# Mixer A's values in plain float32, in pairs of 64-column products, two bursts a unit

## The chip, the cores and the metric

The kernel runs on one core of a Trainium2 chip. The metric is the device time of one execution in microseconds. The engines are TensorE (PE in the profile, with its weight loads as PEld), VectorE (DVE), ScalarE (ACT), GpSimd (POOL) and SyncE (SP, which issues most of the DMAs).

## What is computed

One layer of a hybrid attention model: a normalized and modulated input, one input projection, two attention mixers with eight query heads each (two key/value heads, so a group of four query heads shares one), gates, one output projection and a residual. 1024 latent tokens attend in blocks of 128 queries; 128 context tokens attend to themselves. Cut to the two mixers for latent tokens:

```python
def global_attn_latent(q, k_lat, v_lat, k_ctx, v_ctx):            # mixer A
    k_all = jnp.concatenate([k_ctx, k_lat], axis=1)               # 128 + 1024 keys
    v_all = jnp.concatenate([v_ctx, v_lat], axis=1)
    def one_block(qblk):                                          # 128 queries
        s = jnp.einsum('bqkgd,bskd->bkgqs', qblk, k_all).astype(jnp.float32) * (d ** -0.5)
        p = jax.nn.softmax(s, axis=-1).astype(v_all.dtype)
        return jnp.einsum('bkgqs,bskd->bqkgd', p, v_all)
...
# mixer B: the same over a window of 128 to each side and the context keys, with a sink logit a head
...
def merge_out(o_a, g_a, o_b, g_b, w_out):
    return jnp.concatenate([o_a * jax.nn.silu(g_a), o_b * jax.nn.silu(g_b)], axis=-1) @ w_out
```

Everything is float32.

## The kernel before

Most matmuls here are in float32r, the type of reduced precision. To keep the result near float32, an operand is kept in two float32r parts, a high one (the rounded value) and a low one (what the rounding left); a product then takes three matmuls (high x high, high x low, low x high).

The first 310 us make the modulation (float32 matmuls in 32-column tiles, line 375), the projections, the rotated and normalized queries (stored in DRAM) and the keys and values, which stay in SBUF. `v_hi[:, m]` holds the high parts of mixer m's values, 64 columns a key block and head group; beside them stand 64 columns of ones for mixer A and the low parts for mixer B. `v_lo` holds mixer A's low parts (`put_values`, `split_values`).

Then comes attention, in 36 units `(t, m, g)`: query tile t, mixer m, head group g, in the order A, B, A, B of each tile; units 32 to 35 are the context ("prompt") tile, last of all. A latent unit of mixer A has nine key blocks, one of the prompt has one; a unit of mixer B has three or four. One block is one slot of a list, written out by hand; the main loop takes a slot an iteration and emits, in this order: what was put off to it (`later(n, f)` puts f n iterations on; `tick` runs it), the scores of the slot, row-maximum matmuls (`pmx`, line 941) or mixer B's score matmuls (`sn`) of a coming unit, some output-projection matmuls (`po`, line 1313, 2.5 a slot from the queue `outq`), and the value products of the slot three back (`LAG`). Each engine runs its instructions in the order of emission.

For a mixer A block, `scores` makes `st` (128 keys x 4 heads x 128 queries) in PSUM with two matmuls, its exponentials `pe` on ScalarE, their high part `ph` on ScalarE (line 1221) and the low part `pl` on GpSimd (line 1225; block 4 on VectorE, line 1223). `values` then adds to the unit's PSUM tile `pv` three matmuls of 512 columns (lines 1235, 1237, 1238): values beside ones x `ph`, low values x `ph` into the upper 64 partitions only, values beside ones x `pl`. So partitions 0 to 63 of `pv` have the weighted values, partitions 64 to 127 the softmax sum. After a unit's last block, iterations later by `END_AT`: `inverse` (ScalarE: log and exponential, which gives 1 over the sum), `gated` (VectorE multiplies by it in two 64-partition halves, GpSimd by the gate tile `sgl`), `parts` (the two float32r parts of the result for the output projection). Mixer B's weights are transposed on TensorE (line 1212), and its value products are two matmuls a block.

Of the kernel before, what the change touches and what calls it, by code (L numbers as in the profile page):

```python
# [18 lines left out]
P = 128  # L19
D = 1024  # L20
KT = D // P
HD = 64
# [11 lines left out]
PROMPT_AT = 32  # L34
KS = (0, 1, 4, 5, 2, 3, 6, 7)
PL_DVE = (4,)
# [48 lines left out]
PROMPT_PV = "CCAC"  # L85
PROMPT_PL = ()
LOW_DVE = (-2, -1)
# [11 lines left out]
VC_AT = 4  # L99
# [31 lines left out]
def hybrid_step(ctx, tc, x_prompt, x_sample, cache_k_a, cache_v_a, cache_k_b, cache_v_b,  # L131
# [18 lines left out]
    def later(n, f):  # L150

        agenda.setdefault(now[0] + n, []).append(f)
# [13 lines left out]
    def bank(tag, name):  # L166
        return ps.tile([P, 512], F32, tag=tag, name=name, bufs=BANKS[tag])
# [604 lines left out]
    def split_values(src, j):  # L772

        nc.vector.tensor_tensor(v_lo[:, j : j + 2, :], src[:, 0], v_hi[:, 0, j : j + 2, 0, :], op=ALU.subtract)
        nc.vector.tensor_tensor(v_hi[:, 1, j : j + 2, 1, :], src[:, 1], v_hi[:, 1, j : j + 2, 0, :], op=ALU.subtract)

    with tc.tile_pool(name="kt", bufs=2) as kt:
        W_GB.pools[WRAW : WRAW + 2] = [(kt, 2)] * 2
        sg_tile.append(lambda n: kt.tile([P, 512], F32, tag="kh", name=n))
        for b in range(0, 20, 4):  # L780
            later(4 + b // 2, lambda b=b: nc.gpsimd.tensor_scalar(
                v_hi[:, 0, b : b + 4, 1, :], gain4, 0.0, 1.0, op0=ALU.mult, op1=ALU.add))
        ones = ident_r.bitcast(F32)[64:68].unsqueeze(1)
        for out, n in ((kla[64:68].rearrange("p g b n -> p (g b) n"), 18), (klp[64:68, 0:2], 2)):
            later(ONES_AT, lambda out=out, n=n: nc.vector.tensor_scalar(
                out, ones.to_broadcast([4, n, P]), 0.0, 1.0, op0=ALU.mult, op1=ALU.add))
# [39 lines left out]

        def put_values(src, t):
            j = 2 * t if t else 18
            nc.scalar.copy(v_hi[:, :, j : j + 2, 0, :], src)
            later(1, lambda: split_values(src, j))  # L830

        def key(pk, t, idx):
# [45 lines left out]
                f()  # L878

        put_keys(kc, 0, 0, "c", CACHE_AT)  # L880
        later(VC_AT, lambda: nc.scalar.copy(v_hi[:, :, 0:2, 0, :], vc))
# [296 lines left out]
    def blocks(t, m, g):  # L1178

        if t == 0:  # L1180
            k = (khp[:, g, :], klp[0:68, g, :]) if m == 0 else 0
            return [(k, v_hi[:, m, 18 + g], v_lo[:, 18 + g, :])]
        if m == 0:
            return [((kha[:, g, b, :], kla[:, g, b, :]), v_hi[:, 0, 2 * b + g], v_lo[:, 2 * b + g, :]) for b in range(9)]
        p0, p1_ = window(t)
        at = {p: b + 1 for b, p in enumerate(POS)}
        return [(p - p0, v_hi[:, 1, 2 * at.get(p, 0) + g], None) for p in range(p0, p1_)]

    pvb, og = {}, {}
    nsl = [0]  # L1190
# [2 lines left out]
    def load_gate(i):  # L1193
        if i < NU:
            t, m, g = units[i]
            sgl[i] = w2.tile([P, 2, P], F32, tag="sgl", name=f"sgl{i}")
            h0 = HD * (8 * m + 4 * g)
            nc.sync.dma_start(
                sgl[i], g_dram[h0 : h0 + 4 * HD, P * place(t) : P * place(t) + P].rearrange("(c p) n -> p c n", p=P))

    def parts_tiles(i, b):
        return [w3.tile([P, 512], F32R, tag=n, name=f"{n}{i}_{b}") for n in ("ph", "pl")]

    def scores(i, b, blk):

        t, m, g = units[i]
        s = bank("B", f"st{i}_{b}")
        ph, pl = parts_tiles(i, b)
        if m == 1:
            o = P * blk[0]  # L1210
# [6 lines left out]
        nc.tensor.matmul(s, kh, qtile[i], start=True, stop=False)  # L1217
# [3 lines left out]
        nc.scalar.copy(ph, pe)  # L1221
        if (i - PROMPT_AT in PROMPT_PL) if t == 0 else b in PL_DVE:
            later(1, lambda: nc.vector.tensor_tensor(pl, pe, ph, op=ALU.subtract))
        else:
            nc.gpsimd.tensor_tensor(pl, pe, ph, op=ALU.subtract)  # L1225
        return ph, pl

    def values(i, b, last, blk, ph, pl):
        t, m, g = units[i]
        _, vh, vl = blk  # L1230
        if b == 0:
            pvb[i] = bank(PROMPT_PV[i - PROMPT_AT] if t == 0 else "C", f"pv{i}")
        pv = pvb[i]
        two = vh.rearrange("p s d -> p (s d)")
        nc.tensor.matmul(pv, two, ph, start=(b == 0), stop=False)  # L1235
        if m == 0:
            nc.tensor.matmul(pv[0:64, :], vl, ph, start=False, stop=False)  # L1237
        nc.tensor.matmul(pv, two, pl, start=False, stop=last)  # L1238
        if not last:
            return  # L1240

        v = {}

        def inverse():
            v["rs"] = w2.tile([64, 512], F32, tag="rs", name=f"rs{i}", bufs=1)
            if m == 1:
                nc.scalar.copy(v["rs"], pv[64:128, :])
                return
            nc.scalar.activation(v["rs"], pv[64:128, :], AF.Ln)
            nc.scalar.activation(v["rs"], v["rs"], AF.Exp, scale=-1.0)  # L1250

        def gated():
            rs = v["rs"]
            o = 768 + 256 * (i % 3)
            of = spare[0][:, o : o + 256].rearrange("p (c n) -> p c n", c=2)
            pvv = pv[0:64, :].rearrange("p (c s n) -> p c s n", s=2, n=P)
            srv = rs.rearrange("p (c s n) -> p c s n", s=2, n=P)
            for s in range(2):
                nc.vector.tensor_tensor(of[64 * s : 64 * s + 64], pvv[:, :, s, :], srv[:, :, s, :],
                                        op=ALU.add if m else ALU.mult)  # L1260
            nc.gpsimd.tensor_tensor(of, of, sgl.pop(i), op=ALU.mult)
            later(GATE_LATE, lambda: load_gate(i + 2))
            v["of"] = of

        def parts():
            while held[0] == NOG:
                outq.pop(0)()
            held[0] += 1
            oh = ogp.tile([P, 2, P], F32R, tag="ogh", name=f"ogh{i}")
            ol = ogp.tile([P, 2, P], F32R, tag="ogl", name=f"ogl{i}")  # L1270
            nc.scalar.copy(oh, v["of"])  # L1271
            og[t, 2 * m + g] = oh, ol
            eng = nc.vector if i - PROMPT_AT in LOW_DVE else nc.gpsimd
            later(1, lambda: eng.tensor_tensor(ol, v["of"], oh, op=ALU.subtract))

        ends = PROMPT_END if t == 0 else END_AT if i < PROMPT_AT - 2 else LAST_END
        for n, f in zip(ends, (inverse, gated, parts)):
            later(n, f)
        if m == 1:
            later(ends[3], lambda: outq.extend(out_items(t, g)))  # L1280

    po, yt, gt = {}, {}, {}

# [78 lines left out]
    credit, live = 0.0, []  # L1362
    load_gate(0)
    load_gate(1)
    for s in range(len(slots) + LAG + PROMPT_END[3]):
        tick()
        if s < len(slots):
            live.append((slots[s], slots[s] and scores(slots[s][0], slots[s][1], slots[s][3])))
        for n, at in WO_LATE.items():
            if s == at:  # L1370
                load_wo(n, w2)
                later(3, lambda n=n: split_wo(n))
        for f in due.get(s, ()):
            f()
        for _ in range(LATE[s] if s < len(LATE) else 0):
            late_product(late.pop(0))
        rate = OUTRATE if s < start[PROMPT_AT - HELD] else END_RATE if s < start[PROMPT_AT] else PROMPT_RATE
        credit = min(credit + rate, 6.0) if outq else 0.0
        while outq and credit >= 1.0:
            outq.pop(0)()  # L1380
            credit -= 1.0
        if s >= LAG and live:
            slot, parts = live.pop(0)
            if slot:
                values(*slot, *parts)
    for f in outq:
        f()
    in_order(tc)
# [62 lines left out]
```

## Time and profile before

| | |
|---|---|
| median of three runs | 704.2 us (704.17, 704.20, 704.34) |
| span of the profiled execution | 704.1 us; its own time isn't given apart from the three |
| TensorE busy | 691.6 us, 98% |
| VectorE, ScalarE, GpSimd busy | 443.3, 420.0, 342.3 us |
| attention, 310 to 680 us | TensorE busy 369.2 of 370 us |
| mean granted TensorE clock | 0.997 |

A matmul's time in the profile includes its way through the array, in which the next one already runs: a 512-column float32r matmul has 0.39 us, but the next starts 0.23 us after it. A float32 matmul leaves two records. Lines are those of the kernel before.

### The profile page before, as it was taken

What the parts mean: (1) busy time and instruction counts of PE and PEld (TensorE: products, weight loads), DVE (VectorE), ACT (ScalarE), POOL (GpSimd) and SP (SyncE); (2) the same over time, 40 slices, a digit from 0 to 9 for tenths busy, and PEclk for the clock granted to TensorE, in tenths of its full rate; (3) what the DMA queues carried; (4) which work ended last, traced back from release to release, by engine and by line L of the source; (5) the groups of instructions that cost most, each with busy time, mean ns of one, the idle gap of its engine ahead of it and who ended that gap; (6) DMA issues with size and microseconds to landing.
All of it is one profiled execution on the core that took longest, in us unless ns stands there. A gap on an engine that the chain in (4) does not pass through costs nothing.

```text
span 704.1 us, 10711 instructions
## 1 busy us (share of the span) xinstructions
PE 691.6 (98%) x3554; PEld 561.4 (80%) x3554; DVE 443.3 (63%) x991; ACT 420.0 (60%) x856; POOL 342.3 (49%) x364
## 2 busy tenths in 40 slices
PE   6999999999999999999999999999999999999997
PEld 2788988878788789986788888878888888887876
DVE  3555247875676873537677577667666775775564
ACT  4455411412233553389877877787788778877870
POOL 3457023332323241657857655755574557456742
PEclk9999999999999999999999999999999999999999
DMA  8960283348435015423222122121211231212324
GB/s 330 415 245 16 109 305 76 72 93 295 131 89 175 1 61 187 157 64 102 90 69 83 34 82 73 46 82 58 86 61 52 69 90 46 83 52 90 91 60 144
DMA packets 53447, 78.64 MB, mean 112 GB/s; under 512 B 6848, under 2 KB 25728, under 8 KB 52368
## 3 DMA queue, kind: packets, MB, share of 16 engines
q1 hardware_dynamic: 45360, 66.28, 27.8%
q10 hardware_dynamic: 8032, 11.68, 6.2%
q8 instruction: 28, 0.46, 0.3%
q14 instruction: 27, 0.22, 0.1%
HBM read 58.72 MB, written 19.21 MB: 111 GB/s over the span
## 4 chain that ended last, share of the span: by engine, by line
PE 88%; ACT 4%; DMA 2%; DVE 2%; issue 2%; ACTq 1%; SPq 0%; POOL 0%; DVEq 0%; POOLq 0%
PE po L1313 14%; PE pv L1238 6%; PE pv L1235 6%; PE pmx L941 5%; PE st L1217 4%; PE pv L1237 4%; PE st L1218 4%; PE pq L279 4%; PE pq L280 4%; PE pq L278 4%; PE st L1212 4%; PE pg L292 3%; PE pg L293 3%; PE pg L288 3%; PE pk L279 2%; PE pk L280 2%
## 5 line engine op out<-in xcount | busy, mean ns | idle before, releaser
L1225 POOL TENSOR_TENSOR pl<-pe,ph 128x512 fp32r<-128x512 f32 x130 | 167.9, 1294 | 141.9 <-DVE nm L1002 67.5
L942 DVE TENSOR_REDUCE mx<-pmx 128x1 f32<-128x384 f32 x192 | 101.4, 553 | 57.3 <-PE pmx L941 56.2
L1220 ACT ACTIVATE pe<-st 128x512 f32<-128x512 f32 x146 | 86.7, 594 | 27.1 <-PE st L1218 26.4
L1221 ACT CAST ph<-pe 128x512 fp32r<-128x512 f32 x146 | 90.6, 621 | 4.8
L1238 PE MATMUL pv<-pl,v_hi 128*128 128x512 f32 x208 | 82.5, 397 | 0.3 <-POOL pl L1225 0.3
L1235 PE MATMUL pv<-ph,v_hi 128*128 128x512 f32 x208 | 82.6, 397 | 0.0
L197 POOL TENSOR_TENSOR rs_q<-ms_q,mhalf 128x8 f32<-128x8 f32 x18 | 34.8, 1931 | 80.7 <-DVE ms_q L195 80.7
L1313 PE MATMUL po<-wo,ogh 128*128 128x512 f32 (+1 forms) x224 | 73.1, 387 | 0.0
L1002 DVE CUSTOM_DVE_ANT_0 sn<-sn,mask,nsink 128x512 f32<-128x512 f32 (+1 forms) x64 | 46.4, 724 | 41.0 <-PE sn L999 38.6
L941 PE MATMUL pmx<-kha,qt 128*128 128x384 f32 x192 | 61.0, 363 | 0.5 <-ACT pen L988 0.3
L1217 PE MATMUL st<-qt,kha 128*128 128x512 f32 x144 | 57.9, 402 | 0.1
L1237 PE MATMUL pv<-ph,v_lo 128*64 128x512 f32 x146 | 57.6, 395 | 0.0
L1218 PE MATMUL st<-qb,kla 68*128 68x512 f32 x144 | 57.1, 397 | 0.0
L1238 PEld LDWEIGHTS pv<-pl,v_hi 128*128 128x128 f32 x208 | 39.2, 188 | 17.3 <-POOL pl L1225 0.7
L988 ACT ACTIVATE pen<-sn,nm 128x512 f32<-128x512 f32 (+2 forms) x72 | 44.9, 625 | 5.8 <-DVE nm L1015 2.7
L1213 ACT CAST ph<-st 128x512 fp32r<-128x512 f32 x62 | 36.4, 587 | 19.7 <-PE st L1212 19.4
L1313 PEld LDWEIGHTS po<-wo,ogh 128*128 128x128 f32 x224 | 41.0, 188 | 6.2 <-ACT ogh L1271 0.3
L1235 PEld LDWEIGHTS pv<-ph,v_hi 128*128 128x128 f32 x208 | 39.3, 189 | 7.0 <-issue 0.3
L1313 PE MATMUL po<-wo,ogl 128*128 128x512 f32 (+1 forms) x112 | 43.2, 386 | 0.0
L1214 DVE TENSOR_TENSOR pl<-st,ph 128x512 fp32r<-128x512 f32 x62 | 42.4, 685 | 1.2 <-ACT ph L1213 0.7
L675 ACT ACTIVATE sqq<-pq 128x512 f32<-128x512 f32 x18 | 10.8, 598 | 53.3 <-PE pq L280 13.8
L941 PEld LDWEIGHTS pmx<-kha,qt 128*128 128x128 f32 x192 | 35.5, 190 | 6.4 <-DVE mx L942 1.2
(238 smaller groups left out, 1701.3 us busy)
## 6 DMA issues: line engine op xcount, KB each, us to landing
qt<-qd SPq DMA_DIRECT2D x36, 256.0 KB
wm<-in_w_mod_ss_dram SPq DMA_DIRECT2D x8, 1024.0 KB
qd<-qo0q ACTq DMA_DIRECT2D x36, 128.0 KB
qd<-qo1q ACTq DMA_DIRECT2D x36, 128.0 KB
sgl<-gd SPq DMA_DIRECT2D x36, 128.0 KB
out_dram<-yt SPq DMA_DIRECT2D x17, 256.0 KB
xn<-in_x_sample_dram SPq DMA_DIRECT2D x8, 512.0 KB
wg<-in_w_mod_g_dram SPq DMA_DIRECT2D x4, 1024.0 KB
```

The source lines that it names most:

```text
L941: nc.tensor.matmul(pm[:, 0:384], lhs, kha[:, g, 3 * b : 3 * b + 3, :], start=True, stop=True)
L942: nc.vector.tensor_reduce(mx[:, h, b : b + 1], pm[:, 0:384], axis=AX.X, op=ALU.max)
L1002: nc.vector.tensor_tensor_reduce(s, s, mask[:, m0 : m0 + n], -1.0, nsink[:, 4 * g + h : 4 * g + h + 1], op0=ALU.add, op1=ALU.min, accum_ou ...
L1217: nc.tensor.matmul(s, kh, qtile[i], start=True, stop=False)
L1218: nc.tensor.matmul(s, kl, qbtile[i], start=False, stop=True)
L1220: nc.scalar.activation(pe, s, AF.Exp)
L1221: nc.scalar.copy(ph, pe)
L1225: nc.gpsimd.tensor_tensor(pl, pe, ph, op=ALU.subtract)
L1235: nc.tensor.matmul(pv, two, ph, start=(b == 0), stop=False)
L1237: nc.tensor.matmul(pv[0:64, :], vl, ph, start=False, stop=False)
L1238: nc.tensor.matmul(pv, two, pl, start=False, stop=last)
L1313: nc.tensor.matmul(po[c], x, wo_parts[KT * n + k][lo][:, q], start=(k == KS[0] and p == 0), stop=(k == KS[-1] and p == 2))
```

## The change

Mixer A's values are kept as plain float32 (`v_all`), and a tile of ones beside them; mixer B's parts stay as they were. A mixer A block no longer splits its exponentials: `pe` (seven buffers instead of three) is the moving operand itself. Its value product is a pair of float32 matmuls with the same 64-column weights, one for heads 0 and 2 into partitions 0 to 63 and one for heads 1 and 3 into partitions 64 to 127 of `pv`, 256 columns each. The products of blocks 0 to 4 are emitted together two iterations after block 4's scores (`LAGA`), those of blocks 5 to 8 two after block 8's. The softmax sum is made apart: the blocks' exponentials are added up in a tile `acc` (GpSimd, the last add on VectorE), and one pair with ones as weights, at the end of the second burst, sums that over the keys into the other half of `pv`. So the sums stand on the same partitions as the values; `inverse` works on 128 x 256, GpSimd multiplies the gate by it, and one VectorE multiply of 128 x 256 makes the gated result. A prompt unit of mixer A has one burst of two pairs.

```diff
-PES = 3
+PES = 7
+SPLIT = 5
+LAGA = 2
+ENDA = (1, 3, 5)
+ACC_DVE = (8,)
...
-    v_hi = kv.tile([P, 2, 20, 2, HD], F32R, name="v_hi")
-    v_lo = kv.tile([P, 20, HD], F32R, name="v_lo")
+    v_all = kv.tile([P, 20, HD], F32, name="v_all")
+    v_hi = kv.tile([P, 20, 2, HD], F32R, name="v_hi")
+    ones = kv.tile([P, HD], F32, name="ones")
+    nc.gpsimd.memset(ones, 1.0)
...
+    def keep_values(src, j):
+
+        nc.scalar.copy(v_all[:, j : j + 2, :], src[:, 0])
+        nc.scalar.copy(v_hi[:, j : j + 2, 0, :], src[:, 1])
...
         nc.scalar.activation(pe, s, AF.Exp)
-        nc.scalar.copy(ph, pe)
-        if (i - PROMPT_AT in PROMPT_PL) if t == 0 else b in PL_DVE:
-            later(1, lambda: nc.vector.tensor_tensor(pl, pe, ph, op=ALU.subtract))
+        if b == 0:
+            acc[i] = pe
         else:
-            nc.gpsimd.tensor_tensor(pl, pe, ph, op=ALU.subtract)
-        return ph, pl
+            first = acc[i]
+            if b == 1:
+                acc[i] = w3.tile([P, 512], F32, tag="acc", name=f"acc{i}", bufs=1)
+            add = lambda: (nc.vector if b in ACC_DVE else nc.gpsimd).tensor_tensor(acc[i], first, pe, op=ALU.add)
+            if b in ACC_DVE:
+                later(1, add)
+            else:
+                add()
+        return pe
...
+    def burst(i, made, first, last):
+
+        if first:
+            pvb[i] = pv_bank(i)
+        pv = pvb[i]
+
+        def product(o, lhs, rhs, start, stop):
+            r = rhs.rearrange("p (c s n) -> p c s n", s=2, n=P)
+            for s in range(2):
+                nc.tensor.matmul(pv[HD * s : HD * s + HD, o : o + 256].rearrange("p (c n) -> p c n", c=2), lhs,
+                                 r[:, :, s, :], start=start, stop=stop)
+
+        for n, (blk, pe) in enumerate(made):
+            product(0, blk[1], pe, first and n == 0, False)
+        if not last:
+            return
+        product(256, ones, acc.pop(i), False, True)
+        v = {}
+
+        def inverse():
+            v["rs"] = w2.tile([P, 256], F32, tag="rsa", name=f"rs{i}", bufs=1)
+            nc.scalar.activation(v["rs"], pv[:, 256:512], AF.Ln)
+            nc.scalar.activation(v["rs"], v["rs"], AF.Exp, scale=-1.0)
+            later(1, lambda: nc.gpsimd.tensor_tensor(sgl[i], sgl[i], v["rs"].rearrange("p (c n) -> p c n", c=2),
+                                                     op=ALU.mult))
+
+        def gated():
+            of = place_out(i)
+            nc.vector.tensor_tensor(of, pv[:, 0:256].rearrange("p (c n) -> p c n", c=2), sgl.pop(i), op=ALU.mult)
+            later(GATE_LATE, lambda: load_gate(i + 2))
+            v["of"] = of
+
+        for n, f in zip(ENDA, (inverse, gated, lambda: parts(i, v["of"]))):
+            later(n, f)
...
-        two = vh.rearrange("p s d -> p (s d)")
+        two = blk[1].rearrange("p s d -> p (s d)")
         nc.tensor.matmul(pv, two, ph, start=(b == 0), stop=False)
-        if m == 0:
-            nc.tensor.matmul(pv[0:64, :], vl, ph, start=False, stop=False)
         nc.tensor.matmul(pv, two, pl, start=False, stop=last)
...
         if s < len(slots):
-            live.append((slots[s], slots[s] and scores(slots[s][0], slots[s][1], slots[s][3])))
+            slot = slots[s]
+            made = slot and scores(slot[0], slot[1], slot[3])
+            if slot and units[slot[0]][1] == 0:
+                i, b, last, blk = slot
+                row.setdefault(i, []).append((blk, made))
+                if last or b == SPLIT - 1:
+                    bursts[s + LAGA] = i, row.pop(i), b < SPLIT, last
+                slot = None
+            live.append((slot, made))
...
+        if s in bursts:
+            burst(*bursts.pop(s))
```

TensorE, unit 16 (a mixer A unit in the middle of attention), from block 6's scores on, before: `st16_6` are block 6's scores, `pv16` the unit's value tile, `po4_1` an output tile, `pmx18` the row maxima of the next mixer A unit.

```order
L1217 MATMUL st16_6_5815<-qt16_5196,kha_2344 128x512
L1218 MATMUL st16_6_5815<-qb16_5616,kla_2345 128x512
L1313 MATMUL po4_1_5754<-wo_big0_3635,ogl13_5562 128x512
L1313 MATMUL po4_1_5754<-wo_big0_3635,ogh13_5561 128x512
L1235 MATMUL pv16_5758<-ph16_3_5742,v_hi_2350 128x512
L1237 MATMUL pv16_5758<-ph16_3_5742,v_lo_2351 64x512
L1238 MATMUL pv16_5758<-pl16_3_5743,v_hi_2350 128x512
L1217 MATMUL st16_7_5829<-qt16_5196,kha_2344 128x512
L1218 MATMUL st16_7_5829<-qb16_5616,kla_2345 128x512
L941 MATMUL pmx18_2_2_5838<-kha_2344,qt18_5489 128x384
L941 MATMUL pmx18_3_0_5841<-kha_2344,qt18_5489 128x384
```

And the same place in the changed kernel, where x2 is a pair:

```order
L1226 MATMUL st16_6_5504<-qt16_4966,kha_2344 128x512
L1227 MATMUL st16_6_5504<-qb16_5330,kla_2345 128x512
L1360 MATMUL po4_1_5465<-wo_big0_3601,ogl13_5285 128x512
L1360 MATMUL po4_1_5465<-wo_big0_3601,ogh13_5284 128x512
L1255 MATMUL pv16_5512<-pe16_0_5398,v_all_2350 64x256 x2
L1255 MATMUL pv16_5512<-pe16_1_5417,v_all_2350 64x256 x2
L1255 MATMUL pv16_5512<-pe16_2_5440,v_all_2350 64x256 x2
L1255 MATMUL pv16_5512<-pe16_3_5458,v_all_2350 64x256 x2
L1255 MATMUL pv16_5512<-pe16_4_5473,v_all_2350 64x256 x2
L1226 MATMUL st16_7_5523<-qt16_4966,kha_2344 128x512
L1227 MATMUL st16_7_5523<-qb16_5330,kla_2345 128x512
```

Before, each iteration has the three products of the block three back; now the first burst has five blocks' pairs, and the iterations around it have none.

The end of the unit in the changed kernel, four iterations on (`st17` are the transposed weights of the mixer B unit that follows):

```order
L1221 MATMUL st17_1_5575<-ident_r_100,pen17_5400 128x128 x4
L948 MATMUL pmx20_0_1_5588<-kha_2344,qt20_5480 128x384
L1255 MATMUL pv16_5512<-pe16_5_5487,v_all_2350 64x256 x2
L1255 MATMUL pv16_5512<-pe16_6_5507,v_all_2350 64x256 x2
L1255 MATMUL pv16_5512<-pe16_7_5526,v_all_2350 64x256 x2
L1255 MATMUL pv16_5512<-pe16_8_5545,v_all_2350 64x256 x2
L1255 MATMUL pv16_5512<-acc16_5419,ones_2352 64x256 x2
L1221 MATMUL st17_2_5605<-ident_r_100,pen17_5400 128x128 x4
L948 MATMUL pmx20_0_2_5613<-kha_2344,qt20_5480 128x384
```

The second burst stands in the second slot of the mixer B unit, and its last pair reads `acc16`, the sum of all nine blocks.

GpSimd, the same unit in the changed kernel, from the first add of the sum on (`sgl14` and `sgl15` are gate tiles, `ogl14` the low part of a result, `spare` the gated result):

```order
L1236 TENSOR_TENSOR acc16_5419<-pe16_0_5398,pe16_1_5417 128x512
L1052 TENSOR_TENSOR sgl15_5287<-sgl15_5287,spare_3494 128x256
L1236 TENSOR_TENSOR acc16_5419<-acc16_5419,pe16_2_5440 128x512
L1295 TENSOR_TENSOR ogl14_5432<-spare_3494,ogh14_5431 128x256
L1236 TENSOR_TENSOR acc16_5419<-acc16_5419,pe16_3_5458 128x512
L1236 TENSOR_TENSOR acc16_5419<-acc16_5419,pe16_4_5473 128x512
L1027 TENSOR_TENSOR ex17_5403<-nm17_5401,sink_105 128x4
L1236 TENSOR_TENSOR acc16_5419<-acc16_5419,pe16_5_5487 128x512
L1320 TENSOR_TENSOR spare_3494<-spare_3494,sgl15_5287 128x256
L1041 TENSOR_TENSOR sum17_5402<-sum17_5402,ex17_5403 128x4
L1236 TENSOR_TENSOR acc16_5419<-acc16_5419,pe16_6_5507 128x512
L1236 TENSOR_TENSOR acc16_5419<-acc16_5419,pe16_7_5526 128x512
```

Where each of these adds stands there was a subtraction `pl`, on its own, of the same block; now each add needs the one before it.

More of the change, by code (lines that the diff above doesn't have):

```diff
@@ L779, in hybrid_step @@
         sg_tile.append(lambda n: kt.tile([P, 512], F32, tag="kh", name=n))
[L780 to L783, printed above, removed]
+        some = ident_r.bitcast(F32)[64:68].unsqueeze(1)
         for out, n in ((kla[64:68].rearrange("p g b n -> p (g b) n"), 18), (klp[64:68, 0:2], 2)):
             later(ONES_AT, lambda out=out, n=n: nc.vector.tensor_scalar(
-                out, ones.to_broadcast([4, n, P]), 0.0, 1.0, op0=ALU.mult, op1=ALU.add))
+                out, some.to_broadcast([4, n, P]), 0.0, 1.0, op0=ALU.mult, op1=ALU.add))
         tabs = []
@@ L1181, in blocks @@
             k = (khp[:, g, :], klp[0:68, g, :]) if m == 0 else 0
-            return [(k, v_hi[:, m, 18 + g], v_lo[:, 18 + g, :])]
+            return [(k, (v_hi if m else v_all)[:, 18 + g])]
         if m == 0:
-            return [((kha[:, g, b, :], kla[:, g, b, :]), v_hi[:, 0, 2 * b + g], v_lo[:, 2 * b + g, :]) for b in range(9)]
+            return [((kha[:, g, b, :], kla[:, g, b, :]), v_all[:, 2 * b + g]) for b in range(9)]
         p0, p1_ = window(t)
         at = {p: b + 1 for b, p in enumerate(POS)}
-        return [(p - p0, v_hi[:, 1, 2 * at.get(p, 0) + g], None) for p in range(p0, p1_)]
+        return [(p - p0, v_hi[:, 2 * at.get(p, 0) + g]) for p in range(p0, p1_)]
     pvb, og = {}, {}
@@ new lines, in place_out, with parts @@
+    def place_out(i):
+        o = 768 + 256 * (i % 3)
+        return spare[0][:, o : o + 256].rearrange("p (c n) -> p c n", c=2)
+    def parts(i, of):
+        t, m, g = units[i]
+        while held[0] == NOG:
+            outq.pop(0)()
+        held[0] += 1
+        oh = ogp.tile([P, 2, P], F32R, tag="ogh", name=f"ogh{i}")
+        ol = ogp.tile([P, 2, P], F32R, tag="ogl", name=f"ogl{i}")
+        nc.scalar.copy(oh, of)
+        og[t, 2 * m + g] = oh, ol
+        eng = nc.vector if i - PROMPT_AT in LOW_DVE else nc.gpsimd
+        later(1, lambda: eng.tensor_tensor(ol, of, oh, op=ALU.subtract))
@@ L1263, in gated @@
             v["of"] = of
[L1265 to L1274, printed above, removed]
         ends = PROMPT_END if t == 0 else END_AT if i < PROMPT_AT - 2 else LAST_END
-        for n, f in zip(ends, (inverse, gated, parts)):
+        for n, f in zip(ends, (inverse, gated, lambda: parts(i, v["of"]))):
             later(n, f)
-        if m == 1:
-            later(ends[3], lambda: outq.extend(out_items(t, g)))
+        later(ends[3], lambda: outq.extend(out_items(t, g)))
     po, yt, gt = {}, {}, {}
@@ L1361, in hybrid_step @@
     put(LATE_PUT + 3 * LATE_LAG + 3, load_adaln)
-    credit, live = 0.0, []
+    credit, live, row, bursts = 0.0, [], {}, {}
     load_gate(0)
@@ L1382, in hybrid_step @@
         if s >= LAG and live:
-            slot, parts = live.pop(0)
+            slot, made = live.pop(0)
             if slot:
-                values(*slot, *parts)
+                values(*slot, *made)
+        if s in bursts:
+            burst(*bursts.pop(s))
     for f in outq:
```

32 lines of the change are left out of this document (13 added, 19 removed).

## Prediction

> **What bounds the kernel now.** I read the page first (busy shares and the chain that ended last), then the busy times by stretch, TensorE's waits, and last the timeline at single matmuls. All durations below are from the one profiled execution: its span is 704.1 us, and the three timed runs lie at 704.17 to 704.34 us with a median of 704.2 us, so at most 0.2 us lies around the span, and I count from 704.2.
>
> ```profile
> span 704.1 us, 10711 instructions
> PE 691.6 (98%) x3554; PEld 561.4 (80%) x3554; DVE 443.3 (63%) x991; ACT 420.0 (60%) x856; POOL 342.3 (49%) x364
> PE 88%; ACT 4%; DMA 2%; DVE 2%; issue 2%; ACTq 1%; SPq 0%; POOL 0%; DVEq 0%; POOLq 0%
> 240.00:310.00 70.00, 70.00 (x395) 63.53 (x395) 37.36 (x94) 32.24 (x78) 27.10 (x22) 1.00 0.36 118
> 310.00:680.00 370.00, 369.20 (x1782) 294.60 (x1781) 249.59 (x531) 294.69 (x601) 227.68 (x245) 1.00 0.22 70
> PE pv L1238 <- POOL pl L1225: 0.3, 1, 0.3
> ```
>
> In the stretch rows the columns are length, then busy time of TensorE, its weight loads, VectorE, ScalarE and GpSimd, the granted clock, and DMA. The attention stage is 310 to 680 us. TensorE is busy in 369.2 of its 370 us at the full clock, the chain lies on TensorE for 88% of the span, and in the whole kernel TensorE waits 0.3 us for a GpSimd result in the value products. ScalarE (295 us), VectorE (250) and GpSimd (228) all have room. So what counts is how long TensorE's stream of matmuls is. A busy mean is no price there, since matmuls overlap: the price is the distance from one start to the next.
>
> **What the old value products cost.** The group rows give the counts, the timeline the distances.
>
> ```profile
> L1237 PE MATMUL pv<-ph,v_lo 128*64 128x512 f32 x146 | 57.6, 395 | 0.0
> 450.05 0.39 PE L1235 MATMUL pv<-ph,v_hi 128*128 128x512 f32 x1
> 450.05 0.14 PEld L1237 LDWEIGHTS pv<-ph,v_lo 128*64 128x64 f32 x1
> 450.28 0.39 PE L1237 MATMUL pv<-ph,v_lo 128*64 128x512 f32 x1
> 450.51 0.40 PE L1238 MATMUL pv<-pl,v_hi 128*128 128x512 f32 x1
> 450.75 0.39 PE L1217 MATMUL st<-qt,kha 128*128 128x512 f32 x1
> 452.04 0.39 PE L1235 MATMUL pv<-ph,v_hi 128*128 128x512 f32 x1
> 452.73 0.40 PE L1217 MATMUL st<-qt,kha 128*128 128x512 f32 x1
> ```
>
> Line 1237 runs once per mixer A block, so there are 146 blocks (16 latent units of nine, two prompt units of one). A block's three matmuls take 450.05 to 450.75 = 0.70 us, the next one's 452.04 to 452.73 = 0.69: 0.695 us. Removed: 146 x 0.695 = 101.5 us of TensorE.
>
> **What the new pairs cost.** No 64-column float32 pair is in this trace. The nearest row is the modulation product of the first stage (line 375): plain float32, 256 columns wide as the new ones, in four 32-column tiles side by side.
>
> ```profile
> 26.12 0.39 PE L293 MATMUL pg_f<-h,wloga 128*128 128x512 f32 x1
> 26.35 0.39 PE L288 MATMUL pg_f<-h,whiga 128*128 128x512 f32 x1
> 26.67 0.59 PEld L375 LDWEIGHTS pm<-wm,sil 128*32 128x32 f32 x16 [0.36 <-DVE h L440]
> 26.67 1.07 PE L375 MATMUL pm<-wm,sil 128*32 128x256 f32 x16
> 26.91 0.83 PE L375 MATMUL pm<-wm,sil 128*32 128x256 f32 x12
> 27.12 0.61 PE L375 MATMUL pm<-wm,sil 128*32 128x256 f32 x8
> 27.34 0.40 PE L375 MATMUL pm<-wm,sil 128*32 128x256 f32 x4
> 27.67 0.50 PE L292 MATMUL pg_f<-h,whiga 128*128 128x512 f32 x1
> 28.01 0.40 PE L293 MATMUL pg_f<-h,wloga 128*128 128x512 f32 x1
> ```
>
> The rows of line 375 come from ever later windows: 16 records at 26.67, 12 of them left at 26.91, 8 at 27.12, 4 at 27.34. The code has eight matmuls there, so a float32 matmul is two records. The records start in fours, one per tile, and a round takes (27.34 - 26.67) / 3 = 0.223 us. So column tiles in float32 do run beside each other on this chip, and a pair of the new kernel (two tiles, two records each) should take two rounds: 0.446 us. It has 16 x (9 + 1) + 2 x (1 + 1) = 164 pairs, the "+ 1" being the pair that multiplies the summed exponentials by ones: 164 x 0.446 = 73.1 us.
>
> A burst has a price at its ends. From the start of the matmul ahead of that block (26.35) to that of the second behind it (28.01) are 1.66 us; two plain distances (0.23 each, 26.12 to 26.35) and four rounds (0.89) make 1.35, so 0.31 us goes into going in and out: the weight load of line 375 starts only at 26.67, together with its matmul, where elsewhere it starts a matmul earlier. 32 bursts in latent units and 2 in prompt units: 34 x 0.31 = 10.5 us. The lower bound is nothing, from line 1237: a 64-column tile, its weights loaded at 450.05 under the matmul ahead, and 0.23 us on both sides. The upper bound is twice the measured price, 21 us. I take 0.31, because that row has float32 and several tiles as the bursts have, and line 1237 has neither.
>
> The Trainium skill ("TensorEngine Tiling", Key Properties) says that a change of tiling mode drains TensorE; by that the term is the 10.5 us taken, and by the row of line 1237, which goes from 128 to 64 columns and back without a gap, the trace does not bear it out for every change: then the term is 0 and the time 677.
>
> Net: 101.5 - 73.1 - 10.5 = 17.9 us less of TensorE.
>
> **The other engines.** These rows show what goes and what comes.
>
> ```profile
> L1225 POOL TENSOR_TENSOR pl<-pe,ph 128x512 fp32r<-128x512 f32 x130 | 167.9, 1294 | 141.9 <-DVE nm L1002 67.5 <-ACT ph L1221 60.7 <-POOL pl L1225 11.2
> L1261 POOL TENSOR_TENSOR spare<-spare,sgl 128x256 f32<-128x256 f32 x36 | 26.5, 737 | 3.4 <-DMA sgl<-gd 1.6 <-DVE spare L1259 0.7 <-PE po L1313 0.5
> L1274 POOL TENSOR_TENSOR ogl<-spare,ogh 128x256 fp32r<-128x256 f32 x34 | 25.0, 737 | 0.0
> L1045 POOL TENSOR_TENSOR sgl<-sgl,spare 128x256 f32<-128x256 f32 x16 | 12.2, 761 | 0.0
> L1020 POOL TENSOR_TENSOR ex<-nm,sink 128x4 f32<-128x4 f32 x18 | 3.6, 200 | 1.7 <-DVE nm L1015 1.6
> L1223 DVE TENSOR_TENSOR pl<-pe,ph 128x512 fp32r<-128x512 f32 x16 | 11.1, 697 | 25.4 <-ACT ph L1221 25.4
> L942 DVE TENSOR_REDUCE mx<-pmx 128x1 f32<-128x384 f32 x192 | 101.4, 553 | 57.3 <-PE pmx L941 56.2
> L1221 ACT CAST ph<-pe 128x512 fp32r<-128x512 f32 x146 | 90.6, 621 | 4.8
> L829 ACT CAST v_hi<-pk 128x256 fp32r<-128x256 f32 x9 | 3.5, 383 | 2.2 <-DMA qd<-qo1q 2.2
> ```
>
> ScalarE loses 146 casts (90.6 us). GpSimd does seven running-sum adds a unit where it had eight subtractions of the same shape (1.294 us). VectorE gives up 16 subtractions (0.697) and gets 16 adds of that shape. The end of a unit is one 128x256 multiply on VectorE instead of two on 64 partitions, and one on GpSimd as before. None is on TensorE's path while TensorE is full: worth 0. Ahead of attention, ScalarE copies the values in two pieces instead of one (0.383 us, ten times; a second piece costs at most as much, 4 us), under TensorE's 70.00 busy us of 70; cover gone, those 4 us would show. No DMA is added; the gate loads move two slots forward, on a SyncE queue that no term here waits for.
>
> New is what TensorE waits for: the last pair of a unit needs the whole sum. GpSimd adds in a chain from the second block on. In its order, between the first add and the last, stand seven adds (9.06 us), one multiply of line 1045's kind (0.76), one each of lines 1274 and 1261 (1.47) and two small ones (0.2 each, as line 1020): 11.7 us, then VectorE's add, 0.7: 12.4. Over these ten slots TensorE does about 1.3 us a slot without values (450.75 to 452.04 has scores, row maxima and output products), the first burst (5 x 0.446 + 0.31 = 2.5) and four pairs of the second (1.9): 17.4, less 1.1 until the second block's exponentials are there: 16.3. The sum is ready some 4 us early. If it came late, behind TensorE's last pair would stand the whole stream: the next transposes, row maxima and scores. VectorE's last add is a wait too; behind it stand row-maximum reductions (0.553 us, two buffers ahead) and the low parts of mixer B's weights. The slots between the bursts are short: the eighth has two score and two row-maximum matmuls, about 0.8 us, against two reductions, 1.1 us; two buffers and the burst ahead absorb that. I put 1 us in all on such stalls, between 0 and 16 (1 us a latent unit).
>
> 704.2 - 17.9 + 1 = 687.3, so **687**.
>
> **Rivals.**
> *Pairs do not overlap.* Only the four-tile, 32-column form is shown. If the two 64-column tiles run one after the other, a pair is four records, 0.89 us, and 164 x 0.89 + 10.5 = 156.8 us against 101.5: 55 us slower, 759. It turns into a loss from (101.5 - 10.5) / 164 = 0.555 us a pair. Against it: the fours of line 375. For it: both tiles read the same weights and each reads 128-column runs with gaps, which line 375 does not. The Trainium skill ("FP8 and Floating Point Precision", TensorE Precision Notes) counts four passes for true float32, a rule against the change: eight passes of 256 columns where there were three of 512. Chance 0.12.
> *No price at the ends*, as at line 1237: 704.2 - 28.4 + 1 = 677. Against it: the 0.31 us was float32, as here. Chance 0.10.
> *Waits between bursts.* The other engines meet short slots and then a burst in which they starve; TensorE loses 0.3 to 0.9 us a latent unit, 5 to 14 us on top of 686.3: 691 to 700. For it: the 1.1 against 0.8 us above; against it: VectorE and GpSimd have a third of the stage free, and ScalarE too once its casts are gone. Chance 0.13.
> *The sum is late.* GpSimd's chain would have to be over 4 us longer than counted, and from 5.1 us on (17.9 / 16 past the slack) the gain is gone: about 704. Chance 0.03.
>
> **How the numbers follow.** The forecast case, 683 to 691 (the price at the ends a third more or less, the stalls up to 1 us more or less), has 0.62. The range 676 to 701 takes in the case without the price at the ends and the waits between bursts, 0.85 in all; the serial pairs stay outside. A measurement of this kernel tells about 0.2% (1.4 us) from no change. Faster is 0.62 + 0.10 + 0.12 = 0.84; the same 0.03, from the late sum and the worst waits; slower 0.13, the serial pairs and a sum later still.
>
> **What would show it.** In the new timeline, the records of a burst in twos at 0.22 us, some 2.2 us between the start of a burst's first record and where the sixth pair would begin; the matmul behind it at 0.33 us instead of 0.22 from the last round. The value products of mixer A near 83 us, TensorE still full in the stage, which is about 17 us shorter. Wrong: records of a burst one by one at 0.22 (serial), or TensorE waiting for VectorE's last add of the sum or for row-maximum reductions by more than 5 us in all.

## The result: slower by 1.2%

The changed kernel takes 712.96 us (median of four runs, 711.9 to 714.2) against 704.23 us before: a ratio of 1.0124, 95% interval 1.0110 to 1.0139. I had forecast 687 and a range of 676 to 701. The profiled run is the one of 711.9 us.

The page of the changed kernel, then its attention stage (length, then busy time of TensorE, weight loads, VectorE, ScalarE, GpSimd), the new value products by group, and TensorE's wait for the row maxima in the whole span (total, number of waits, longest). The last row is the row-maximum matmul of the kernel before, whose waits for VectorE come to 0.2 us:

```profile
span 710.1 us, 10894 instructions
PE 684.7 (96%) x3772; PEld 528.8 (74%) x3772; DVE 429.7 (61%) x963; ACT 324.3 (46%) x720; POOL 316.6 (45%) x342
PE 82%; DVE 6%; DMA 3%; issue 3%; POOL 2%; ACT 2%; ACTq 1%; SPq 0%; DVEq 0%; POOLq 0%
310.00:680.00 370.00, 355.99 (x1959) 258.07 (x1956) 235.08 (x510) 196.58 (x443) 203.46 (x226) 1.00 0.22 70
L1255 PE MATMUL pv<-pe,v_all 128*64 128x256 f32 x584 | 70.5, 385 | 0.0
PE pmx L948 <- DVE mx L949: 7.8, 9, 1.4
L941 PE MATMUL pmx<-kha,qt 128*128 128x384 f32 x192 | 61.0, 363 | 0.5 <-ACT pen L988 0.3 <-DVE mx L942 0.2
```

TensorE was busy in 369.2 of 370 us of this stage; now it is in 356.0, and VectorE, which was 2% of the chain, is 6%. The 7.8 us are above the 5 us that the prediction named as a sign of being wrong. The busy figure still flatters TensorE, since a matmul counts as busy until its end is through the array, and a wait of up to 0.16 us hides under that. The distances between starts show more. Here is one mixer A unit's first burst and what follows, on TensorE:

```profile
473.66 0.40 PE L1360 MATMUL po<-wo_big,ogh 128*128 128x512 f32 x1
473.98 2.38 PE L1255 MATMUL pv<-pe,v_all 128*64 128x256 f32 x20
476.29 0.50 PE L1226 MATMUL st<-qt,kha 128*128 128x512 f32 x1
476.63 0.39 PE L1227 MATMUL st<-qb,kla 68*128 68x512 f32 x1
478.59 0.60 PE L1221 MATMUL st<-ident_r,pen 128*128 128x128 f32 x4
480.10 0.44 PE L948 MATMUL pmx<-kha,qt 128*128 128x384 f32 x1 [0.92 <-DVE mx L949]
480.65 0.27 PE L1056 MATMUL pti<-ident_r,inv 128*4 128x128 f32 x1
480.76 0.60 PE L1221 MATMUL st<-ident_r,pen 128*128 128x128 f32 x4
481.27 0.44 PE L948 MATMUL pmx<-kha,qt 128*128 128x384 f32 x1
481.63 1.95 PE L1255 MATMUL pv<-pe,v_all 128*64 128x256 f32 x16
483.41 0.60 PE L1255 MATMUL pv<-acc,ones 128*64 128x256 f32 x4
483.94 0.55 PE L1221 MATMUL st<-ident_r,pen 128*128 128x128 f32 x3
```

The pairs do overlap, and a burst costs what I had said. Five pairs are 20 records. From the start of the matmul ahead (473.66) to the second behind (476.63) are 2.97 us; less two plain distances of 0.23 that is 2.51, against a forecast of 5 x 0.446 = 2.23 for the pairs and 0.31 for the ends, 2.54. How the 2.51 divides shows in run e8 (below), whose bursts of three pairs last 1.45 us from the first record to the matmul behind (446.58 to 448.03) where these of five last 2.31 (473.98 to 476.29): 0.43 us a pair, and so about 0.35 for the ends. The 32 bursts of the latent units take 80 us, where their 144 blocks of old products took 144 x 0.695 = 100.

But behind the burst TensorE stands still. The four transposes at 478.59 (0.108 us each) are through by 479.02; the row-maximum matmul starts at 480.10, 1.08 us late, and the transpose at 480.65 follows it by 0.55 us where 0.175 are due. VectorE in the same stretch:

```profile
473.22 0.84 DVE L1319 TENSOR_TENSOR spare<-pv,rs 64x256 f32<-64x256 f32 x2
477.23 1.02 DVE L949 TENSOR_REDUCE mx<-pmx 128x1 f32<-128x384 f32 x2 [3.17 <-PE pmx L948]
478.17 0.69 DVE L1365 TENSOR_TENSOR po<-po,wo_big 128x512 f32<-128x512 f32 x1
478.89 0.69 DVE L1366 TENSOR_TENSOR yt<-po,yt 128x512 f32<-128x512 f32 x1
479.50 1.01 DVE L949 TENSOR_REDUCE mx<-pmx 128x1 f32<-128x384 f32 x2
480.43 0.17 DVE L1044 RECIPROCAL inv<-sum 128x4 f32<-128x4 f32 x1
480.51 0.66 DVE L1236 TENSOR_TENSOR acc<-acc,pe 128x512 f32<-128x512 f32 x1
481.09 0.55 DVE L949 TENSOR_REDUCE mx<-pmx 128x1 f32<-128x384 f32 x1
```

While the burst runs, VectorE has nothing to read: it sits idle for 3.17 us until the first row maxima behind the burst come. Then its whole backlog arrives at once, two reductions, a tile's output multiply and add, two more reductions, and it works without a gap from 477.23 on. The row-maximum products have two buffers, and the next matmul of that kind waits until VectorE has read one of them. Every second unit has the output multiply and add there. Before the change VectorE's longest idle time in the same place was 1.29 us:

```profile
451.59 1.02 DVE L942 TENSOR_REDUCE mx<-pmx 128x1 f32<-128x384 f32 x2 [1.29 <-PE pmx L941]
```

The length of a steady unit is the start of block 0's scores to that of the next mixer A unit. Ten units lie between the first row and the second of each kernel (before, then changed):

```profile
365.33 0.43 PE L1217 MATMUL st<-qt,kha 128*128 128x512 f32 x1
603.95 0.43 PE L1217 MATMUL st<-qt,kha 128*128 128x512 f32 x1
```

```profile
366.32 0.47 PE L1226 MATMUL st<-qt,kha 128*128 128x512 f32 x1
607.53 0.47 PE L1226 MATMUL st<-qt,kha 128*128 128x512 f32 x1
```

A mixer A unit with its mixer B unit took 23.86 us before and takes 24.12 now. By the prices measured above it should take 23.86 - 9 x 0.695 + 2 x 2.51 = 22.63. (The second burst costs up to 0.1 us more than the first: 481.27 to 483.94, less the 0.175 of the matmul ahead, against 473.66 to 476.29, less 0.23. So 22.63 is good to about 0.1.) So about 1.5 us of waiting a unit, some 24 us if all 16 latent units wait alike, ate the saving of 20 us and some more. Of the 8.7 us lost, the steady units account for about 4, at 0.26 us each. From the first unit's first scores to the third's the changed kernel takes 41.40 us against 38.89, 2.5 more, and from the last mixer A unit's first scores on latent queries to the end 56.8 us against 55.2, 1.6 more.

### The profile page after: what moved, and what is told of

The parts are those of the page before. It is cut to its first block, busy times and chain, and to the rows that moved or that the text cites. A ratio compares the mean times of both kernels' runs of the same rounds, so it can differ in the third digit from the quotient of the medians.

```text
span 710.1 us, 10894 instructions
## 1 busy us (share of the span) xinstructions
PE 684.7 (96%) x3772; PEld 528.8 (74%) x3772; DVE 429.7 (61%) x963; ACT 324.3 (46%) x720; POOL 316.6 (45%) x342
## 4 chain that ended last, share of the span: by engine, by line
PE 82%; DVE 6%; DMA 3%; issue 3%; POOL 2%; ACT 2%; ACTq 1%; SPq 0%; DVEq 0%; POOLq 0%
PE po L1360 13%; PE pv L1255 10%; PE st L1226 5%; PE pmx L948 4%; PE st L1227 4%; PE pq L283 4%; PE pq L284 4%; PE pq L282 4%; PE st L1221 3%; PE pg L292 3%; PE pg L297 3%; PE pg L296 3%; PE pk L283 2%; PE pk L284 2%; DVE mx L949 2%
## 5 line engine op out<-in xcount | busy, mean ns | idle before, releaser
L1236 POOL TENSOR_TENSOR acc<-acc,pe 128x512 f32<-128x512 f32 x96 | 123.0, 1281 | 24.2 <-ACT pe L1229 21.0
L948 PE MATMUL pmx<-kha,qt 128*128 128x384 f32 x192 | 63.7, 377 | 8.6 <-DVE mx L949 7.8
L1255 PE MATMUL pv<-pe,v_all 128*64 128x256 f32 x584 | 70.5, 385 | 0.0
L1226 PE MATMUL st<-qt,kha 128*128 128x512 f32 x144 | 60.4, 419 | 2.2 <-DVE pl L1223 1.1
L1255 PEld LDWEIGHTS pv<-pe,v_all 128*64 128x64 f32 x584 | 38.9, 136 | 25.3 <-issue 9.0
L1236 POOL TENSOR_TENSOR acc<-pe,pe 128x512 f32<-128x512 f32 x16 | 20.6, 1285 | 70.5 <-ACT pe L1229 70.5
L1269 POOL TENSOR_TENSOR sgl<-sgl,rs 128x256 f32<-128x256 f32 x18 | 13.2, 735 | 69.0 <-ACT rs L1268 65.8
L1226 PEld LDWEIGHTS st<-qt,kha 128*128 128x128 f32 x144 | 27.0, 188 | 19.5 <-issue 9.7
L1221 PE MATMUL st<-ident_r,pen 128*128 128x128 f32 x248 | 38.4, 277 | 0.8 <-DVE pen L1046 0.7
L445 POOL TENSOR_TENSOR h<-hf,h 128x256 fp32r<-128x256 f32 (+2 forms) x33 | 28.2, 870 | 20.1 <-DVE h L444 20.1
```

The source lines that it names most:

```text
L948: nc.tensor.matmul(pm[:, 0:384], lhs, kha[:, g, 3 * b : 3 * b + 3, :], start=True, stop=True)
L1236: add = lambda: (nc.vector if b in ACC_DVE else nc.gpsimd).tensor_tensor(acc[i], first, pe, op=ALU.add)
L1255: nc.tensor.matmul(pv[HD * s : HD * s + HD, o : o + 256].rearrange("p (c n) -> p c n", c=2), lhs, r[:, :, s, :], start=start, stop=stop)
```

## The experiments

Theory 1: TensorE waits for VectorE between the bursts. Theory 2: TensorE's own work costs more than counted. Theory 3: the running sum is late. "Unit" in the table is the length of a steady unit, taken as above from ten units; the ratios are to the kernel before, run on the same chip.

| run | us | ratio (95%) | unit, us |
|---|---|---|---|
| before | 704.2 to 704.5 | | 23.86 |
| changed | 712.96 | 1.0124 (1.0110 to 1.0139) | 24.12 |
| e1 changed, short reductions | 702.03 | 0.9967 (0.9954 to 0.9980) | 23.17 |
| e2 before, short reductions | 702.70 | 0.9976 (0.9967 to 0.9985) | 23.80 |
| e3 1.9 output matmuls a slot | 711.34 | 1.0102 (1.0085 to 1.0119) | 24.00 |
| e4 last add on GpSimd | 711.23 | 1.0096 (1.0079 to 1.0113) | 24.13 |
| e5 row maxima in slot 6 | 709.57 | 1.0068 (1.0050 to 1.0086) | 23.70 |
| e6 e5 and 2.75 a slot | 705.21 | 1.0010 (0.9996 to 1.0024) | 23.42 |
| e7 e5 and last add on GpSimd | 704.70 | 1.0002 (0.9992 to 1.0012) | 23.70 |
| e8 three bursts | 710.17 | 1.0081 (1.0062 to 1.0100) | 24.00 |
| e9 e6 and last add on GpSimd | 701.32 | 0.9961 (0.9949 to 0.9974) | 23.43 |
| e10 e9 and a later transpose | 698.06 | 0.9917 (0.9903 to 0.9930) | 23.16 |
| e11 2.75 a slot alone | 711.15 | 1.0101 (1.0081 to 1.0120) | 23.91 |
| e12 e10, short reductions | 691.61 | 0.9819 (0.9803 to 0.9836) | 22.76 |

### Less work on VectorE, TensorE's the same (e1, e2)

```diff
-                nc.vector.tensor_reduce(mx[:, h, b : b + 1], pm[:, 0:384], axis=AX.X, op=ALU.max)
+                nc.vector.tensor_reduce(mx[:, h, b : b + 1], pm[:, 0:128], axis=AX.X, op=ALU.max)
```

> The changed kernel, but each row-maximum reduction on VectorE reads 128 of its 384 columns, so that the maximum that shifts the exponentials leaves out part of the keys (the TensorE work is the same). By the two widths in the trace of before (384 columns 0.553 us, 12 columns 0.15 us) one should take about 0.28 us, so VectorE loses some 3.3 us a mixer A unit. Theory 1, TensorE waits for VectorE in the short slots between bursts (about 1.3 us a latent unit in the trace): most of these waits go, 690 to 697 us. Theory 2, the time went into TensorE itself (the bursts' ends or the float32 pairs cost more than counted): no change, 711 to 714 us. Theory 3, the sum is late: nearly no change, since the sum hangs on GpSimd's chain, 708 to 714 us.

> The kernel before, with the same cut of the row-maximum reductions to 128 of 384 columns. TensorE waited for nearly nothing there, so every theory has 703 to 704.5 us; below 702 would say that VectorE had already been a bound before the change.

The same cut takes 10.9 us off the changed kernel and 1.7 off the one before. In both it leaves TensorE's instructions as they were, so theory 2 can't explain the 10.9; theory 3 had allowed 5 at most. It is less than the 16 to 23 us that theory 1 expected: a unit still has 0.5 us more than 22.63, and the first two units are no faster for it (19.49 and 22.92 us against 19.58 and 21.82). The control moved a little below its 703, though not below 702: VectorE was hardly a bound before the change (0.06 us a unit).

### Where the work stands, not how much (e3, e5, e6, e11)

```diff
-OUTRATE = 2.5
+OUTRATE = 1.9
```

> The changed kernel with output-projection matmuls emitted at 1.9 a slot instead of 2.5 (24 of them stand behind each mixer B unit and 13 slots lie between, 1.85 a slot), so that they also fill the slots ahead of the second burst, which had none. No engine gets more or less work. Theory 1 (waits for VectorE in short slots): the same VectorE work meets longer slots, 0.5 to 1.3 us a latent unit less waiting: 692 to 705 us. Theory 2 (TensorE's own cost): 711 to 714 us. Theory 3 (late sum): the second burst comes later by two or three output matmuls, so some gain, 706 to 712 us.

```diff
-MX_AT = (-4, -3, -2, -2, -1, 4, 5, 5, 7, 7, 8, 8)
+MX_AT = (-4, -3, -2, -2, -1, 4, 5, 5, 6, 6, 7, 8)
```

> The changed kernel with two of a unit's twelve row-maximum matmuls moved from slots 7 and 8 to slot 6, just ahead of the first burst (slots 7 and 8 keep one each). No work is added or taken away. Theory 1 in its sharper form, VectorE is left without input during the first burst (3.17 us idle in the trace) and is then late for the matmuls behind it: VectorE reduces these two during the burst, and the waits behind it lose about 1 us a pair of units at least, 0.5 to 1 us a latent unit: 697 to 706 us. Rival, VectorE's sum of work outside the bursts is too much wherever it stands: 709 to 714 us.

The next run has e5's edit and `OUTRATE = 2.75`; e11 has the rate alone.

> As the run before, and the output-projection matmuls at 2.75 a slot instead of 2.5, so that a tile's last output matmul falls into slot 6, and its multiply and add on VectorE (1.4 us) into the first burst too. Theory 1 (VectorE starves in the burst): no slower than the run before, 695 to 705 us. Rival (too much VectorE work in sum): 709 to 714. If short slots without output matmuls are what counts: slower than the run before by 2 to 5 us.

> The changed kernel with output matmuls at 2.75 a slot alone (row maxima as in the changed kernel), so that only a tile's last multiply and add on VectorE come into the first burst. By theory 1 the 1.1 us wait of every second unit goes, and the others stay: 704 to 709 us. If filling the short slots is what counts: slower than the changed kernel, 713 us or more.

Filling the short slots with output matmuls (e3) gave 1.6 us, a miss for theory 1, in the ranges of theories 2 and 3, and less than the runs of the changed kernel differ among themselves. By the distances in its trace, the waits left the slots ahead of the second burst and came up in the slots behind it, which then were short. Feeding VectorE ahead of the burst did more for the steady units: with two row maxima in slot 6 (e5) a unit lost 0.4 us, and with the last output matmul in that slot too (e6) another 0.3. Yet the time of e5, 709.57 us, is a miss too, and lies where the rival had put it (709 to 714): its first two units took 43.1 us together, 1.7 more than in the changed kernel, which hid part of the gain. e6, at 705.21, ends just above theory 1's 705 and clear of the rival's range. VectorE and TensorE around a first burst in e6:

```profile
449.51 0.84 DVE L1319 TENSOR_TENSOR spare<-pv,rs 64x256 f32<-64x256 f32 x2
450.38 1.02 DVE L949 TENSOR_REDUCE mx<-pmx 128x1 f32<-128x384 f32 x2
453.89 1.20 DVE L949 TENSOR_REDUCE mx<-pmx 128x1 f32<-128x384 f32 x2 [2.49 <-PE pmx L948]
455.82 1.20 DVE L1236 TENSOR_TENSOR acc<-acc,pe 128x512 f32<-128x512 f32 x1 [0.65 <-POOL acc L1236]
```

```profile
450.63 2.38 PE L1255 MATMUL pv<-pe,v_all 128*64 128x256 f32 x20
452.94 0.50 PE L1226 MATMUL st<-qt,kha 128*128 128x512 f32 x1
454.42 0.66 PE L1221 MATMUL st<-ident_r,pen 128*128 128x128 f32 x4
454.83 0.42 PE L948 MATMUL pmx<-kha,qt 128*128 128x384 f32 x1
455.22 0.27 PE L1056 MATMUL pti<-ident_r,inv 128*4 128x128 f32 x1
```

Two reductions now start at 450.38 and run into the burst; the row-maximum matmul behind the transposes starts 0.41 us after them, without the 1.08 us, and every unit has the same length. VectorE still has 2.49 us without input there, but it no longer makes TensorE late at this matmul. The total work of each engine is as in the changed kernel, so the rival "too much VectorE work wherever it stands" is out for this part, the 0.7 us a unit that moving work gave. The rate alone (e11) made the units equal at 23.91 us, a fifth of a microsecond shorter, but 711.15 us is a miss of the 704 to 709 expected: its first two units were as slow as those of e5.

### The sum (e4, e7)

```diff
-ACC_DVE = (8,)
+ACC_DVE = ()
```

> The changed kernel with the last add of the running sum on GpSimd (1.28 us there) instead of VectorE (0.7 to 0.85 us), so VectorE has one operation less right ahead of the second burst. Theory 1: 0.3 to 0.85 us a latent unit less waiting, 699 to 708 us. Theory 2: 711 to 714 us. Theory 3 (late sum): GpSimd's chain gets longer, the last pair waits more, 714 to 722 us.

> As the first run of this set, and the last add of the sum on GpSimd. On its own that add's move left the steady units as they were and shortened the first two by some 2 us; expected 0 to 3 us under the first run of this set by theory 1; if the sum is late instead (theory 3), 3 us or more above it.

e4 is 1.7 us faster, no more than the runs of the changed kernel differ, and in theory 2's range. The steady unit stays as it was (24.13 us, and 23.70 in e7), so the expectation for e4 was missed: VectorE's last add does not hold TensorE up there. On top of e5, though, it is worth 4.9 us (more than the 0 to 3 expected), on top of e6 3.9 (e9), and it lies in the first units: the first two take 43.1 us in e5 and 38.8 in e7. VectorE, then TensorE, at the first unit's end in the changed kernel:

```profile
314.53 1.07 DVE L1236 TENSOR_TENSOR acc<-acc,pe 128x512 f32<-128x512 f32 x1 [0.81 <-POOL acc L1236]
315.53 0.55 DVE L949 TENSOR_REDUCE mx<-pmx 128x1 f32<-128x384 f32 x1
```

```profile
316.13 0.45 PE L948 MATMUL pmx<-kha,qt 128*128 128x384 f32 x1 [0.69 <-DVE mx L949]
318.28 0.60 PE L1255 MATMUL pv<-acc,ones 128*64 128x256 f32 x4
```

VectorE waits 0.81 us at its last add for GpSimd's chain, the add itself takes 1.07, and the reduction queued behind it starts only at 315.53; TensorE's next row-maximum matmul waits 0.69 us for that. So a late sum did cost time, but not at the pair that reads it: at the operations queued behind the add on VectorE.

### Three bursts (e8)

```diff
-SPLIT = 5
+SPLIT = (2, 5)
...
-                if last or b == SPLIT - 1:
-                    bursts[s + LAGA] = i, row.pop(i), b < SPLIT, last
+                if last or b in SPLIT:
+                    bursts[s + LAGA] = i, row.pop(i), b in (0, SPLIT[0]), last
```

> The changed kernel with three bursts a latent unit (blocks 0 to 2, 3 to 5, 6 to 8 and the sum) instead of two; row maxima as in the changed kernel. One more pair of burst ends is 0.27 to 0.31 us a unit, 4.3 to 5 us in all. Theory 2 (ends and pairs cost TensorE more than counted): 716 to 722 us. Theory 1 (VectorE starved by long bursts): shorter bursts starve it less, so the waits give back 0.2 to 0.8 us a unit: 703 to 714 us.

2.8 us faster than the changed kernel, though TensorE has 16 more bursts' ends (5.6 us at 0.35). The waits gave back more than the ends cost, which speaks against theory 2 again. A single burst a unit was not run, nor a third buffer for the row-maximum products.

### What adds up (e9, e10, e12)

e9 has the edits of e6 and e4. e10 also has

```diff
-ROWS_AT = (1, 1, 4, 6)
+ROWS_AT = (2, 2, 5, 6)
```

and e12 is e10 with e1's short reductions.

> All three edits together: two row-maximum matmuls in slot 6, 2.75 output matmuls a slot, the last add of the sum on GpSimd. By theory 1 the gains add up, since they lie in different places: 705.2 us with the first two, less the 4 us by which the third shortened the first two units: 700 to 703 us, below the kernel before. Rival (GpSimd's longer chain makes the sum late once the slots are shorter): 705 us or more.

> As the run before, with the transpose of mixer B's inverse sums put behind the second burst instead of ahead of it (one slot later, and the load of its rows one slot later), where it waited 0.21 to 0.37 us for VectorE in each unit. By theory 1 that wait goes: 0 to 5 us under the run before, 696 to 702 us. If VectorE is late anyway, the wait moves to the row-maximum matmul behind it: no change.

> The kernel of run e10 (698.1 us) with each row-maximum reduction reading 128 of 384 columns, which leaves out part of the keys from the shift of the exponentials, as in e1. In the kernel before the same cut took 1.7 us, in the changed kernel 11. If the three edits have taken VectorE off TensorE's path for the most part, only 2 to 4 us are left to gain: 694 to 696 us. If VectorE is still what is late: 688 to 693 us.

e10 beats both kernels: 698.06 us, 0.9917 of the kernel before (0.9903 to 0.9930), by four constants that move work and add none. Its transpose of mixer B's inverse sums now stands behind the second burst, without a wait ahead of it. TensorE from the matmul behind a first burst to the next first burst, e10, then e12:

```profile
447.95 0.50 PE L1226 MATMUL st<-qt,kha 128*128 128x512 f32 x1
450.64 0.42 PE L948 MATMUL pmx<-kha,qt 128*128 128x384 f32 x1
450.99 1.95 PE L1255 MATMUL pv<-pe,v_all 128*64 128x256 f32 x16
452.77 0.60 PE L1255 MATMUL pv<-acc,ones 128*64 128x256 f32 x4
453.30 0.27 PE L1056 MATMUL pti<-ident_r,inv 128*4 128x128 f32 x1
468.81 2.38 PE L1255 MATMUL pv<-pe,v_all 128*64 128x256 f32 x20
```

```profile
444.89 0.50 PE L1226 MATMUL st<-qt,kha 128*128 128x512 f32 x1
447.93 1.95 PE L1255 MATMUL pv<-pe,v_all 128*64 128x256 f32 x16
450.24 0.27 PE L1056 MATMUL pti<-ident_r,inv 128*4 128x128 f32 x1
465.35 2.38 PE L1255 MATMUL pv<-pe,v_all 128*64 128x256 f32 x20
```

e12 took another 6.5 us off, and at 691.61 us it lies where its expectation had put "VectorE is still what is late" (688 to 693). So the four edits have not taken VectorE off TensorE's path. The rows show where it still stands: from the first burst to the second both kernels take 3.04 us, but from the matmul behind the second burst to the next first burst e10 takes 15.51 us and e12 15.11. The 0.40 us a unit lie behind the second burst, and the edits that move work had left them there: in the changed kernel the same cut takes 0.39 us from that stretch (14.64 us, in e1 14.25, means of nine units).

In e12, with the reductions short as well, a unit is 22.76 us, 0.13 above the 22.63 without waits. So in the steady units the difference between 24.12 and 22.63 is TensorE waiting for VectorE, nearly all of it: 0.96 us went by moving work (e10), 0.40 by shorter reductions, and 0.13 is left, about what 22.63 is uncertain by. e12 at 691.6 is 5 us above the forecast without its 1 us of stalls (686.3); 2 of these are the 0.13 a unit, and the rest, in the first units and the tail, was not taken apart.

## Why the prediction was wrong

**Right:** the bound (TensorE's stream), the price of the old products, the overlap of the 64-column pairs, and the price of a burst with its ends (2.51 us measured, 2.54 forecast; the pair is a little cheaper than 0.446 and the ends a little dearer than 0.31). The rivals "pairs do not overlap" and "no price at the ends" are both refuted by the burst's rows. The Trainium skill ("TensorEngine Tiling", Key Properties) says that a change of tiling mode drains TensorE. The bursts agree, with 0.35 us for going in and out, though no run shows that a drain is what takes this time.

**The step that failed** is the term "I put 1 us in all on such stalls, between 0 and 16". It was about 1.5 us a latent unit, some 24 in all. The reason that I gave, "two buffers and the burst ahead absorb that", had the burst's effect the wrong way round. I took a burst as time in which VectorE catches up. But VectorE's work comes from TensorE's results, through two buffers, and during the first burst TensorE makes none: VectorE runs dry (3.17 us) and has less time for the same work outside. I had compared one short slot's reductions with its matmuls; I should have asked what VectorE still has to do when a burst begins, and what stands in its queue behind the burst. VectorE's rows behind the burst show it: the output multiply and add and four reductions close together. The starved burst is not the whole of it: some 0.4 us a unit was lost behind the second burst, and e12 shows that it went only when VectorE had less work.

**The rivals.** "Waits between bursts" was the right one, at 0.3 to 0.9 us a unit too cheap, with a chance of 0.13, and not seen as a case that could end on the slow side. Its argument "VectorE and GpSimd have a third of the stage free" was a mean over the stage: outside the bursts VectorE is free only where its input lets it be. "The sum is late" was counted at the wrong place: no row of the changed kernel shows the last pair waiting (in the unit above the sum is ready at 481.17, some 2 us ahead of it, where I had counted 4), but the reductions behind VectorE's last add did wait, in the first units. The prediction had named that add as a wait with reductions behind it, and given it no term of its own.

**A smaller one:** a run's time is 1.7 to 1.9 us above its span in every run that has both (711.9 against 710.1), not at most 0.2. The profiled execution of before, with a span of 704.1, was thus one of about 705.9 us, above the median.

## What to carry to other kernels

When matmuls are gathered into a burst, list for every engine that reads TensorE's results what it has left to do when the burst starts; where that is less than the burst, the engine runs dry, and TensorE may wait for it behind the burst (here 3.17 us and 1.08), whatever its mean share says. Put matmuls whose results feed that engine just ahead of the burst, and keep its long operations out of the stretch just behind. A wait on one engine is paid by what is queued behind the waiting instruction, so place a step that waits for a slow chain (here the last add of the sum) on the engine that owns the chain.

## What the runs showed of the hardware

Float32 products of 64 columns and 256 moving columns, in two tiles, run side by side at 0.43 us a pair, two rounds of 0.22, as the four 32-column tiles did. TensorE's busy time missed, by estimate, about 10 of the 24 us of waits (14 of 370 us appeared idle in the stage), since short ones disappear under the tail of the matmul before: the transpose at 480.65 was 0.38 us late, and only 0.11 of that is a gap between the rows. VectorE's short reductions in e12, by group:

```profile
L949 DVE TENSOR_REDUCE mx<-pmx 128x1 f32<-128x128 f32 x192 | 51.6, 287 | 110.5 <-PE pmx L948 110.3
```

A reduction's time shrinks less than its width: 128 columns take 287 ns where 384 take 0.55 us (the row at 481.09 above).
